# An output projection by one Strassen level, in two contraction phases, in a hybrid attention and pooling block

## The chip, the cores and the metric

The kernel runs on one core of one Trainium2 chip. The metric is the device time of one execution in microseconds; three runs of the kernel before gave 2625.17, 2625.77 and 2626.29, median 2625.77. A profiled execution of it, from which all rows below are taken, has a span of 2626.6 us.

## What is computed

One layer over 512 tokens of width 4096. A normalised input goes through one input projection; its columns feed a sparse attention (16 heads over a shared latent, the keys picked by an indexer) and a pooling mixer (4 groups). Each branch is multiplied by its own gate; the two are put side by side (4096 channels), go through the output projection, and the normalised result is added to the input:

```python
h = _rmsnorm(x, pre_norm[l])
z = jnp.einsum('bsd,de->bse', h, w_in[l])
q, c, qi, kix, wix, gate_a, pool_in, gate_b = _split_cols(z)
...
ya = _sparse_attention(q, c, qi, kix, wix, w_uk[l], w_uv[l], k_top).reshape(B, S, D_ATTN)
ya = ya * jax.nn.silu(gate_a)
yb = _multiscale_pool(pool_in, w_pool[l], pool_scale[l]) * jax.nn.silu(gate_b)
y = jnp.einsum('bse,ed->bsd', jnp.concatenate([ya, yb], axis=-1), w_out[l])
x = x + _rmsnorm(y, post_norm[l])
```

The output projection is the einsum with `w_out`: 512 x 4096 times 4096 x 4096.

## The kernel before

All large products are made in a split form. `split` (L57) writes a float32 tile as a high part (ACT cast) and a low part (DVE subtraction, source minus high part); `mm3` (L70) makes a product of two such pairs by three matmuls, high by high, high by low and low by high. `staged` (L61) loads a 128 x 512 tile of weights from HBM by the SP queue and splits it, four buffers deep.

Stages in order: a first projection of the latent and the indexer keys, while the normalised input `xh`, `xl` (32 row tiles of 512 tokens) is written to SBUF and kept; then groups of 128 output channels (`group`, L235), each 8 steps `q` of one staged tile and 12 matmuls of 512 moving columns. Between the steps the helper `bg` emits pieces of other work (indexer, top k, attention, mixer). Each finished 128-channel tile goes by `put` (L334) to `cat` in HBM; the last one stays in SBUF. The very last group is the gate of the pooling mixer, group 3, part 3, with 12 matmuls of the mixer's own map (`ymix`) among its 96.

The output projection stands in the last pool scope (L481 on). `reload` brings the 32 tiles of `cat` back and splits them into `ch`, `cl`, which take the SBUF places of `xh`, `xl`. `chunk(db, blocks)` handles 512 output columns: for each of 32 row tiles `e` it stages `wout[db, e]` and makes three matmuls for each block of 128 tokens. The tokens are the stationary side (128 columns), the weights the moving side (512 columns). The first five chunks do all four token blocks, the others two and two, so that blocks 0 and 1 can be normalised and stored (`finish`) while blocks 2 and 3 are still multiplied. At the end of a chunk ACT squares the result with a running sum (L506, `junk`), DVE multiplies it by the post norm (L509, `yg`). `fetch` loads x, `finish` computes the root of the mean and does the last multiply-add (L530) and the store (L531).

A scheduler in the tile framework sets the order of the instructions on each engine from the program, so the order of the code is not the order on an engine; each engine then runs its own list in order, waiting at semaphores. Weight loads of TensorE (rows PEld) stand beside the matmuls (rows PE).

Of the kernel before, what the change touches and what calls it, by code (L numbers as in the profile page):

```python
# [43 lines left out]
def block_kernel(ctx: ExitStack, tc: tile.TileContext, xT, x, gk, wc, wkw, wf, wuk, wuv, kvn,  # L44
# [44 lines left out]
    cat = dr.tile([NK, P, S], F32, name="cat")  # L89

# [144 lines left out]
    def group(gi, evac, per=1, t0=0):  # L235
# [98 lines left out]
    def put(e, src, scl, sg):  # L334
        V.scalar_tensor_tensor(sg, src, scl, sg, op0=ALU.mult, op1=ALU.mult)
        if e == NK - 1:
            split(sg, *[t[:, 1] for t in cat_tile(NK // 2 - 1)])
# [4 lines left out]

    def cat_tile(i):
        if i not in ct:
            ct[i] = (big.tile([P, 2, S], F32R, tag=f"h{i}", name=f"ch{i}"),
                     big.tile([P, 2, S], F32R, tag=f"l{i}", name=f"cl{i}"))
        return ct[i]

    def pool_group(pl, g):
# [36 lines left out]
        for d in range(4):  # L386
# [8 lines left out]
            group(G_GB + 4 * g + d, evac, 2 if d == 0 else 1)  # L395
# [84 lines left out]

    with tc.tile_pool(name="op", bufs=2, reuse_waits="tile") as opl:  # L481
        def reload(i):
            for j in range(2):
                if 2 * i + j < NK - 1:
                    raw = st.tile([P, S], F32, tag="raw", name="cat_raw")
                    nc.sync.dma_start(raw, cat[2 * i + j])
                    split(raw, *[t[:, j] for t in cat_tile(i)])

        yss = [opl.tile([P, 8], F32, name=f"yss{b}", bufs=1) for b in range(NB)]
        yg = {}  # L490

        def chunk(db, blocks, every=1):
            pg = opl.tile([P, 512], F32, name="pg", bufs=1)
            nc.sync.dma_start(pg, gpost[:, ts(db, 512)].to_broadcast([P, 512]))
            yp = [bank("acc" if i == 3 else "w") for i in range(len(blocks))]
            for e in range(NK):
                if db == 0 and e % 2 == 0 and e // 2 + 2 < NK // 2:
                    reload(e // 2 + 2)
                wo = staged(wout[db, e])
                for i, b in enumerate(blocks):  # L500
                    mm3(yp[i], tuple(t[:, e % 2, ts(b, P)] for t in ct[e // 2]), wo, e == 0, e == NK - 1)
                if e % every == 0:
                    bg.step()
            for i, b in enumerate(blocks):
                junk = opl.tile([P, 512], mybir.dt.bfloat16, name="junk", bufs=1)
                A.activation(junk, yp[i], AF.Square, accum_out=yss[b][:, db:db + 1])  # L506
                tag, n = ("yb", 2 * NFULL) if b >= 2 and db < NFULL else ("ya", 16)
                yg[b, db] = opl.tile([P, 512], F32, tag=tag, name="yg", bufs=n)
                V.tensor_mul(yg[b, db], yp[i], pg)  # L509

        xs = {}
# [108 lines left out]
```

## Time and profile before

| | before |
|---|---|
| median of 3 runs | 2625.77 us |
| span of the profiled execution | 2626.6 us |
| PE busy | 2587.6 us (99%), 11768 matmuls |
| PEld busy | 2147.4 us (82%) |
| DVE busy | 1176.9 us (45%) |
| ACT busy | 863.8 us (33%) |
| output projection, first to last matmul | 1902.45 to 2609.93 us |
| HBM traffic | 293.53 MB read, 16.52 MB written |

The page gives busy time by engine, the chain of work that ended last, and groups of instructions by line. A matmul's end is modelled and matmuls overlap, so their pace is read from the distance of their starts and not from their length. A wait matters where TensorE stands behind it; idle time of DVE or ACT by itself costs nothing.

### The profile page before, as it was taken

To read this page: it belongs to the slowest core of one execution; us is meant where nothing else is said; L and a number is where in the kernel's file an instruction comes from. 1 tells how busy PE (TensorE), PEld (TensorE's weight loads), DVE (VectorE), ACT (ScalarE), POOL (GpSimd) and SP (SyncE) were. 2 spreads that over 40 slices of the span, in tenths; PEclk is the share of its full clock that TensorE was granted. 3 is DMA by queue.
4 is the path that set the end of the run, shared out by engine and by line. 5 is a ranking of instruction groups with operands and counts; after the bars stand their busy time and mean duration, and the time that the engine had idled before them with its cause. 6 is when DMAs were issued, how large, how long until landed. Compare 5 with 4: busy or idle time off the path is not lost.

```text
span 2626.6 us, 31765 instructions
## 1 busy us (share of the span) xinstructions
PE 2587.6 (99%) x11768; PEld 2147.4 (82%) x11768; DVE 1176.9 (45%) x2086; ACT 863.8 (33%) x1542; POOL 46.7 (2%) x36
## 2 busy tenths in 40 slices
PE   7999999999999999999999999999999999999997
PEld 5799888888888888888888888888888888888875
DVE  9465783344344444444344334344452222235655
ACT  5344322233333333333332222222342222235443
POOL 5100000000000000000000000000000000000000
PEclk9999999999999999999999999999999999999998
DMA  6334333333333333333333333333473333346786
GB/s 202 99 100 109 96 100 107 103 92 90 98 94 92 89 97 92 92 93 92 94 93 97 106 106 96 105 104 101 129 224 101 101 97 103 101 133 197 224 284 220
DMA packets 169068, 312.15 MB, mean 119 GB/s; under 512 B 19536, under 2 KB 19664, under 8 KB 168912
## 3 DMA queue, kind: packets, MB, share of 16 engines
q1 hardware_dynamic: 168912, 310.12, 40.5%
q8 instruction: 92, 1.51, 0.2%
q14 instruction: 64, 0.52, 0.1%
HBM read 293.53 MB, written 16.52 MB: 118 GB/s over the span
## 4 chain that ended last, share of the span: by engine, by line
PE 90%; DMA 2%; DVE 1%; ACT 0%; issue 0%; DVEq 0%; SPq 0%; ACTq 0%
PE ps_acc L72 21%; PE ps_acc L74 20%; PE ps_acc L73 20%; PE ps_w L73 9%; PE ps_w L74 9%; PE ps_w L72 9%; DMA raw<-in_wout 2%; PE ps_w L447 1%; PE ps_w L279 1%; DVE lo L59 0%; DVE xr L530 0%; DMA xr<-in_x 0%; ACT hi L58 0%; DMA out<-xr 0%; DVE yg L509 0%
## 5 line engine op out<-in xcount | busy, mean ns | idle before, releaser
L59 DVE TENSOR_TENSOR lo<-raw,hi 128x512 fp32r<-128x512 f32 x1008 | 698.7, 695 | 1216.7 <-ACT hi L58 1143.2
L58 ACT CAST hi<-raw 128x512 fp32r<-128x512 f32 x1008 | 626.2, 622 | 1548.4 <-PE ps_acc L73 929.1
L72 PE MATMUL ps_acc<-xh,hi 128*128 128x512 f32 (+1 forms) x2304 | 893.0, 388 | 0.0
L74 PE MATMUL ps_acc<-xh,lo 128*128 128x512 f32 (+1 forms) x2304 | 883.9, 384 | 0.0
L73 PE MATMUL ps_acc<-xl,hi 128*128 128x512 f32 (+1 forms) x2304 | 883.7, 384 | 0.0
L72 PEld LDWEIGHTS ps_acc<-xh,hi 128*128 128x128 f32 x2304 | 432.7, 188 | 81.5 <-issue 2.2
L74 PEld LDWEIGHTS ps_acc<-xh,lo 128*128 128x128 f32 x2304 | 432.4, 188 | 81.4 <-issue 0.2
L73 PEld LDWEIGHTS ps_acc<-xl,hi 128*128 128x128 f32 x2304 | 433.0, 188 | 76.3
L73 PE MATMUL ps_w<-lo,ch 128*128 128x512 f32 x864 | 338.3, 392 | 3.3 <-DVE lo L59 3.2
L72 PE MATMUL ps_w<-hi,ch 128*128 128x512 f32 x864 | 337.2, 390 | 1.8 <-ACT hi L58 1.8
L74 PE MATMUL ps_w<-hi,cl 128*128 128x512 f32 x864 | 336.9, 390 | 0.0
L73 PEld LDWEIGHTS ps_w<-lo,ch 128*128 128x128 f32 x864 | 162.6, 188 | 41.8 <-DVE lo L59 8.3
L72 PEld LDWEIGHTS ps_w<-hi,ch 128*128 128x128 f32 x864 | 162.5, 188 | 36.7 <-ACT hi L58 2.7
L74 PEld LDWEIGHTS ps_w<-hi,cl 128*128 128x128 f32 x864 | 162.6, 188 | 33.4
L73 PE MATMUL ps_w<-lo,xh 128*128 128x512 f32 x128 | 52.9, 414 | 9.6 <-DVE lo L59 9.6
L72 PE MATMUL ps_acc<-hi,ch 128*128 128x512 f32 x160 | 62.2, 389 | 0.0
L73 PE MATMUL ps_acc<-lo,ch 128*128 128x512 f32 x160 | 62.2, 389 | 0.0
L74 PE MATMUL ps_acc<-hi,cl 128*128 128x512 f32 x160 | 62.2, 389 | 0.0
L72 PE MATMUL ps_w<-hi,xh 128*128 128x512 f32 x128 | 52.5, 410 | 7.1 <-ACT xh L58 6.4
L426 ACT ACTIVATE prob<-prob,nm 128x128 f32<-128x128 f32 (+1 forms) x64 | 36.1, 564 | 63.3 <-DVE nm L423 63.3
L74 PE MATMUL ps_w<-hi,xl 128*128 128x512 f32 x128 | 52.2, 408 | 0.0
L155 POOL TENSOR_TENSOR sumsq<-sumsq,sq 128x512 f32<-128x512 f32 x31 | 45.9, 1481 | 34.0 <-ACT sq L151 32.8
(180 smaller groups left out, 1601.3 us busy)
## 6 DMA issues: line engine op xcount, KB each, us to landing
raw<-in_wf SPq DMA_DIRECT2D x576, 256.0 KB, 2.6
raw<-in_wout SPq DMA_DIRECT2D x352, 256.0 KB, 2.9
raw<-in_wc SPq DMA_DIRECT2D x32, 256.0 KB, 2.7
xr<-in_x SPq DMA_DIRECT2D x32, 256.0 KB, 4.7
out<-xr SPq DMA_DIRECT2D x32, 256.0 KB, 2.3
cat_raw<-cat SPq DMA_DIRECT2D x31, 256.0 KB, 2.9
xt<-in_xT SPq DMA_DIRECT2D x15, 512.0 KB, 3.6
raw<-in_wpool SPq DMA_DIRECT2D x16, 256.0 KB, 2.6
```

Of the source, the lines that this page charges most:

```text
L58: A.copy(hi, src)
L59: V.tensor_sub(lo, src, hi.bitcast(F32))
L72: nc.tensor.matmul(dst, lh, rh, start=start, stop=False)
L73: nc.tensor.matmul(dst, lh, rl, start=False, stop=False)
L74: nc.tensor.matmul(dst, ll, rh, start=False, stop=stop)
L155: nc.gpsimd.tensor_add(sumsq, sumsq, sq)
L279: nc.tensor.matmul(dp[j][:, :n], lhs[j][x0], rhs[j][x1], start=i == 0, stop=i == 2)
L426: A.activation(pb, pb, AF.Exp, scale=-1.0, bias=nm, accum_out=sm)
L447: nc.tensor.transpose(tp[:, ts(b - s, P)], prob[:, OFF[b] + P * s:OFF[b] + P * s + P], ident)
```

## The change

The output projection is replaced. Tokens (512 = 2 x 256), contraction rows (pairs of 128-row tiles) and columns (512 = 2 x 256) are each cut in halves, and the 2 x 2 by 2 x 2 block product is made by 7 products of sums of blocks (one Strassen level, Winograd's form) in place of 8. The 16 pairs of row tiles are taken in two phases of 9 and 7 pairs (`KP`): phase 0 pairs tiles 0 to 8 with 9 to 17, phase 1 pairs 18 to 24 with 25 to 31. A phase goes over all 8 blocks of 512 columns.

- `operands(p, i)` loads two tiles of `cat`, makes four sums on DVE (256 columns each) and splits all seven operands into one tile `ops`, which lies where part of the normalised input was. For phase 0, `operands` 0 to 7 are emitted among the steps of the last group (`after`), the ninth behind it; for phase 1 in the last block of phase 0.
- `weights(p, db, i)` loads a 128 x 1024 tile of the four quadrants of `w_out`, makes four sums on DVE (512, 256 and 256 columns) and splits seven operands (512 and 1280 columns), two buffers deep, two steps ahead.
- A step is 7 products x 2 halves of 128 tokens x 3 matmuls of 256 moving columns into 7 PSUM banks. After the last step of a block ACT copies the banks to `pt`, and `collect` adds them up on DVE, spread over the next steps by `bg`. In phase 0 POOL stores the block to `part` in HBM; in phase 1 POOL adds the stored block back by two accumulating transfers (256 KB, then 768 KB), then ACT squares eight pieces (L564) and DVE scales.
- x is loaded in tiles of 128 x 2048 at the end of phase 1; the root and the last multiply-add stand behind the last `collect`, for all tokens; stores are 1 MB each.
- `put` writes every tile to `cat`; the input is kept in tiles of seven slots (`x_slot`) instead of pairs. The pool `st` is closed before the projection. On the host `wout` and `x` are laid out by quadrants.

```diff
-            h2 = big.tile([P, 2, S], F32R, tag=f"h{k2}", name=f"xh{k2}")
-            l2 = big.tile([P, 2, S], F32R, tag=f"l{k2}", name=f"xl{k2}")
...
-                split(gx, h2[:, j], l2[:, j])
-                xh.append(h2[:, j])
-                xl.append(l2[:, j])
+                xh.append(x_slot(2 * k))
+                xl.append(x_slot(2 * k + 1))
+                split(gx, xh[k], xl[k])
...
             if q == 7:
                 evac(z)
+            if after:
+                after(q)
             bg.step(per)
...
+    def operands(p, i, pool, tag=None, bufs=1):
+        e = 2 * (KP[0] * p) + i
+        w = pool.tile([P, 8, H], F32, tag=tag, name="cw", bufs=bufs)
+        q, s = w[:, 0:4], w[:, 4:8]
+        for j in range(2):
+            nc.sync.dma_start(q[:, 2 * j:2 * j + 2], cat[e + KP[p] * j].rearrange("p (a t) -> p a t", a=2))
+        V.tensor_add(s[:, 0], q[:, 1], q[:, 3])
+        V.tensor_sub(s[:, 2], q[:, 0], q[:, 1])
+        V.tensor_sub(s[:, 1], s[:, 0], q[:, 0])
+        V.tensor_sub(s[:, 3], q[:, 2], s[:, 1])
+        o = big.tile([P, 2, NSLOT // 2, H], F32R, tag=f"k{i}", name=f"ops{i}")
+        split(w[:, 0:3:2], o[:, 0, 0:2], o[:, 1, 0:2])
+        split(w[:, 3:8], o[:, 0, 2:7], o[:, 1, 2:7])
+        cat_ops[p, i] = o
...
+        def weights(p, db, i):
+            w = opl.tile([P, 8, H], F32, name="wr")
+            nc.sync.dma_start(w[:, 0:4], wout[KP[0] * p + i, db].rearrange("p (a c) -> p a c", a=4))
+            V.tensor_sub(w[:, 4:6], w[:, 1:3], w[:, 0:2])
+            V.tensor_sub(w[:, 6], w[:, 2], w[:, 4])
+            V.tensor_sub(w[:, 7], w[:, 3], w[:, 6])
+            hi = opl.tile([P, 7, H], F32R, name="wh")
+            lo = opl.tile([P, 7, H], F32R, name="wl")
+            split(w[:, 0:3:2], hi[:, 0:2], lo[:, 0:2])
+            split(w[:, 3:8], hi[:, 2:7], lo[:, 2:7])
+            return hi, lo
...
+            V.tensor_add(c0, pt[:, 0:1], pt[:, 1:2])
+            V.tensor_add(pt[:, 2], pt[:, 2], pt[:, 0])
+            yield
+            V.tensor_add(c[:, 0:2], pt[:, 3:5], pt[:, 2:3].to_broadcast([P, 2, 512]))
+            yield
+            V.tensor_add(c[:, 2], c[:, 0], pt[:, 4])
+            V.tensor_add(c[:, 0:2], c[:, 0:2], pt[:, 5:7])
+            yield
+            if p == 0:
+                nc.gpsimd.dma_start(part[db], t)
+                return
+            nc.gpsimd.dma_start(c0, part[db, :, 0:1], accum_op=ALU.add)
+            nc.gpsimd.dma_start(c, part[db, :, 1:4], accum_op=ALU.add)
...
+                A.activation(junk, slot[:, ts(i % 2, H)], AF.Square, accum_out=yss[:, i, db:db + 1])
...
+        order = [(p, db, i) for p in range(2) for db in range(NG) for i in range(KP[p])]
+        operands(0, 8, opl, "yo", 3)
+        staged_w = {n: weights(*order[n]) for n in range(2)}
+        for n, (p, db, i) in enumerate(order):
...
+            for (a, w), z in zip(PRODUCTS, banks):
+                for h in range(2):
+                    zz, ab = z[:, ts(h, H)], (o[:, 0, a, ts(h, P)], o[:, 1, a, ts(h, P)])
+                    nc.tensor.matmul(zz, ab[0], wh[:, w], start=i == 0 and h == 0, stop=False)
+                    nc.tensor.matmul(zz, ab[0], wl[:, w], start=False, stop=False)
+                    nc.tensor.matmul(zz, ab[1], wh[:, w], start=False, stop=i == KP[p] - 1 and h == 1)
+            if i == KP[p] - 1:
+                pt = opl.tile([P, 7, 512], F32, name="pt", bufs=1)
+                for j, z in enumerate(banks):
+                    A.copy(pt[:, j], z)
+                bg.add(collect(p, db, pt))
+            if n + 2 < len(order):
+                staged_w[n + 2] = weights(*order[n + 2])
+            if p == 0 and db == NG - 1 and i < KP[1]:
+                operands(1, i, opl, "yo", 3)
+            bg.step()
```

The list of PE is the same in both programs up to the first matmul of the projection. Three places on the engines that feed it follow; `raw`, `hi`, `lo` are a staged weight tile and its parts, `wr`, `wh`, `wl` the same of the changed kernel (one number per step), `cw` and `ops` the sources and parts of the operands.

DVE where the last group ends (`gate_z` is its result), before:

```order
L59 TENSOR_TENSOR cl3_15256<-cat_raw_15253,ch3_15255 128x512
L59 TENSOR_TENSOR cl3_15256<-cat_raw_15259,ch3_15255 128x512
L59 TENSOR_TENSOR lo_15266<-raw_15263,hi_15265 128x512
L330 TENSOR_TENSOR gate_z_15163<-ps_acc_14999,R_72 128x512
L59 TENSOR_TENSOR lo_15284<-raw_15281,hi_15283 128x512
L59 TENSOR_TENSOR cl4_15302<-cat_raw_15299,ch4_15301 128x512
L332 SCALAR_TENSOR_TENSOR sg_15162<-sg_15162,gate_z_15163 128x512
L59 TENSOR_TENSOR cl4_15302<-cat_raw_15305,ch4_15301 128x512
L335 SCALAR_TENSOR_TENSOR sg_15162<-ps_w_14998,psc_75,sg_15162 128x512
```

The same engine behind the gate, now, down to the first low part of the first step's weights:

```order
L63 TENSOR_TENSOR ops7_15239<-cw_15232,ops7_15239 128x512
L63 TENSOR_TENSOR ops6_15202<-cw_15195,ops6_15202 128x1280
L363 TENSOR_TENSOR cw_15232<-cw_15232 128x256
L63 TENSOR_TENSOR ops7_15239<-cw_15232,ops7_15239 128x1280
L361 TENSOR_TENSOR cw_15251<-cw_15251 128x256
L360 TENSOR_TENSOR cw_15251<-cw_15251 128x256
L362 TENSOR_TENSOR cw_15251<-cw_15251 128x256
L63 TENSOR_TENSOR ops8_15258<-cw_15251,ops8_15258 128x512
L363 TENSOR_TENSOR cw_15251<-cw_15251 128x256
L511 TENSOR_TENSOR wr_15263<-wr_15263 128x512
L63 TENSOR_TENSOR wl_15269<-wr_15263,wh_15268 128x512
```

Before, weights of the projection were split ahead of the gate; now operands 6 to 8 stand between the gate and the first weights.

ACT in the projection before, over the end of a chunk:

```order
L58 CAST hi_16557<-raw_16555 128x512
L58 CAST hi_16575<-raw_16573 128x512
L506 ACTIVATE junk_16515,yss0_15177<-ps_w_15935 128x512
L506 ACTIVATE junk_16519,yss1_15178<-ps_w_15936 128x512
L506 ACTIVATE junk_16523,yss2_15179<-ps_w_15937 128x512
L506 ACTIVATE junk_16527,yss3_15180<-ps_acc_15938 128x512
L58 CAST hi_16593<-raw_16591 128x512
```

ACT now, in the last block of phase 0, with the operands of phase 1:

```order
L62 CAST wh_18961<-wr_18956 128x512
L62 CAST ops2_18974<-cw_18967 128x512
L62 CAST wh_19027<-wr_19022 128x512
L62 CAST wh_18961<-wr_18956 128x1280
L62 CAST ops3_19040<-cw_19033 128x512
L62 CAST ops2_18974<-cw_18967 128x1280
L62 CAST wh_19092<-wr_19087 128x512
L62 CAST wh_19027<-wr_19022 128x1280
```

The casts of the operands stand between those of the weights, and twice the small cast of a step stands ahead of the large cast of the step before it.

ACT now, behind the end of a block of phase 1 (`k9` and `y0` are the results that the accumulating transfers write):

```order
L62 CAST wh_20155<-wr_20150 128x512
L62 CAST wh_20155<-wr_20150 128x1280
L564 ACTIVATE junk_20497,yss_15250<-k9_20222 128x256
L564 ACTIVATE junk_20499,yss_15250<-k9_20222 128x256
L62 CAST wh_20216<-wr_20211 128x512
L62 CAST wh_20216<-wr_20211 128x1280
L62 CAST wh_20272<-wr_20267 128x512
L564 ACTIVATE junk_20501,yss_15250<-y0_19747 128x256
L62 CAST wh_20272<-wr_20267 128x1280
L564 ACTIVATE junk_20503,yss_15250<-y0_19747 128x256
```

The squares read what a transfer wrote, and casts of later weights stand behind them; before, they read PSUM.

## Rows read from the trace of the kernel before

**Rows 1.** Page: busy us, share and count by engine; the chain's shares.

```profile
PE 2587.6 (99%) x11768; PEld 2147.4 (82%) x11768; DVE 1176.9 (45%) x2086; ACT 863.8 (33%) x1542; POOL 46.7 (2%) x36
PE 90%; DMA 2%; DVE 1%; ACT 0%; issue 0%; DVEq 0%; SPq 0%; ACTq 0%
```

**Rows 2.** Stages: us, busy of PE, PEld, DVE, ACT, POOL; clock; DMA.

```profile
1902.45:2450.00 547.55, 547.55 (x2417) 453.41 (x2416) 200.97 (x295) 181.66 (x317) 0.00 (x0) 1.00 0.47 135
2450.00:2609.93 159.93, 154.85 (x658) 123.07 (x656) 88.34 (x143) 71.63 (x123) 0.00 (x0) 0.99 0.78 246
2609.93:2626.60 16.67, 0.00 (x1) 0.00 (x0) 13.41 (x32) 1.14 (x5) 0.00 (x0) 0.57 0.65 252
```

**Rows 3.** Timeline of PE in the projection (start, length, what), 45 intervals apart.

```profile
2189.64 0.39 PE L73 MATMUL ps_w<-lo,ch 128*128 128x512 f32 x1
...
2199.84 0.39 PE L73 MATMUL ps_w<-lo,ch 128*128 128x512 f32 x1
```

**Rows 4.** Timeline of PE, then of PEld, in the attention.

```profile
516.65 0.28 PE L72 MATMUL ps_w<-kh,qh 128*128 128x256 f32 x1
516.77 0.28 PE L73 MATMUL ps_w<-kl,qh 128*128 128x256 f32 x1
516.89 0.28 PE L74 MATMUL ps_w<-kh,ql 128*128 128x256 f32 x1
517.01 0.40 PE L72 MATMUL ps_acc<-xh,hi 128*128 128x512 f32 x1
517.24 0.40 PE L73 MATMUL ps_acc<-xl,hi 128*128 128x512 f32 x1
...
516.77 0.19 PEld L74 LDWEIGHTS ps_w<-kh,ql 128*128 128x128 f32 x1
516.89 0.19 PEld L72 LDWEIGHTS ps_acc<-xh,hi 128*128 128x128 f32 x1
```

**Rows 5.** DVE groups by form: busy us, mean ns | idle before.

```profile
L59 DVE TENSOR_TENSOR lo<-raw,hi 128x512 fp32r<-128x512 f32 x1008 | 698.7, 695 | 1216.7 <-ACT hi L58 1143.2 <-PE ps_w L447 34.6 <-PE ps_w L73 33.5
L530 DVE SCALAR_TENSOR_TENSOR xr<-yg,ry,xr 128x512 f32<-128x512 f32 x32 | 22.7, 746 | 8.2 <-DMA xr<-in_x 8.2
L229 DVE TENSOR_TENSOR kd<-kt,ib 128x256 f32<-128x256 f32 x2 | 0.8, 424 | 0.1
```

**Rows 6.** Timeline of DVE: two instructions that do not depend on each other.

```profile
1853.45 0.69 DVE L330 TENSOR_TENSOR gate_z<-ps_acc,R 128x512 f32<-128x512 f32 x1 [1.60 <-PE ps_acc L74]
1854.06 0.68 DVE L59 TENSOR_TENSOR lo<-raw,hi 128x512 fp32r<-128x512 f32 x1
```

**Rows 7.** ACT groups by form.

```profile
L58 ACT CAST hi<-raw 128x512 fp32r<-128x512 f32 x1008 | 626.2, 622 | 1548.4 <-PE ps_acc L73 929.1 <-PE ps_acc L74 278.3 <-issue 89.0
L506 ACT ACTIVATION_READ_ACCUMULATOR junk<-ps_w 128x1 f32 x27 | 5.2, 194 | 0.0
L58 ACT CAST kwh<-kwr 128x640 fp32r<-128x640 f32 x4 | 2.9, 722 | 0.0
```

**Rows 8.** DMA issues (KB each, us to landing); landing times of `xr`.

```profile
raw<-in_wout SPq DMA_DIRECT2D x352, 256.0 KB, 2.9
xt<-in_xT SPq DMA_DIRECT2D x15, 512.0 KB, 3.6
...
DMA to landing us min/median/max: 2.0/4.2/6.9
```

**Rows 9.** Timeline of PE at a wait, and the stage behind it.

```profile
2573.52 0.50 PE L72 MATMUL ps_w<-hi,ch 128*128 128x512 f32 x1 [1.64 <-ACT hi L58]
...
2574.60:2577.40 2.80, 2.80 (x8) 2.22 (x7) 1.59 (x3) 1.80 (x3) 0.00 (x0) 0.52 0.82 244
```

**Rows 10.** Timeline of the tail.

```profile
2610.75 0.69 DVE L509 TENSOR_TENSOR yg<-ps_w,pg 128x512 f32<-128x512 f32 x1
...
2612.74 0.75 DVE L530 SCALAR_TENSOR_TENSOR xr<-yg,ry,xr 128x512 f32<-128x512 f32 x1
...
2613.52 10.34 SPq L531 DMA_DIRECT2D out<-xr  x16
```

More of the change, by code (lines that the diff above doesn't have):

```diff
@@ L89, in block_kernel, with x_slot @@
     cat = dr.tile([NK, P, S], F32, name="cat")
+    part = dr.tile([NG, P, 4, 512], F32, name="part")
+    slots = {}
+    def x_slot(i):
+        t, j = divmod(i, NSLOT // 2)
+        if t not in slots:
+            n = min(NSLOT // 2, 2 * NK - i)
+            slots[t] = big.tile([P, n, S], F32R, tag=f"k{t}", name=f"xk{t}")
+        return slots[t][:, j]
     xh, xl = [], []
@@ L233, in block_kernel, with group @@
         split(tp, *kT)
-    def group(gi, evac, per=1, t0=0):
+    def group(gi, evac, per=1, t0=0, after=None):
         z = bank("acc")
@@ L394, in evac @@
                 put(16 + 4 * g + d, yp, psc[:, 4 * g + d:4 * g + d + 1], sg)
-            group(G_GB + 4 * g + d, evac, 2 if d == 0 else 1)
+            last = g == 3 and d == 3
+            group(G_GB + 4 * g + d, evac, 2 if d == 0 else 1,
+                  after=(lambda q: operands(0, q, pl, "cw", 2)) if last else None)
     V.tensor_scalar(psc, psc, 0.5, None, op0=ALU.mult)
@@ L479, in block_kernel @@
     inner.close()
+    st_stack.close()
     with tc.tile_pool(name="op", bufs=2, reuse_waits="tile") as opl:
[L482 to L509, printed above, removed]
@@ L551, in block_kernel @@
[L551 to L557 removed]
+        PRODUCTS = ((0, 0), (1, 2), (4, 5), (5, 4), (3, 3), (2, 6), (6, 1))
+        def weights(p, db, i):
[9 more added lines that the diff above has]
+            return hi, lo
@@ new lines, in block_kernel @@
+        xs = []
+        for db in range(NG):
+            pool, tag, n = (big, f"k{db + 1}", 1) if db < 6 else (opl, "wr", 2)
+            xs.append(pool.tile([P, 4, 512], F32, tag=tag, name=f"xr{db}", bufs=n))
+            nc.sync.dma_start(xs[db], x[db])
+        bg.drain()
+        ry = opl.tile([P, 2, 2], F32, name="ry", bufs=1)
+        ms = opl.tile([P, 2, 2], F32, name="yms", bufs=1)
+        ysum = opl.tile([P, 8], F32, name="ysum", bufs=1)
+        V.tensor_reduce(ysum, yss, axis=AX.X, op=ALU.add)
@@ new lines, in block_kernel @@
+        tot = ysum.rearrange("p (a b) -> p a b", a=2)
+        V.tensor_add(ms, tot[:, 0].rearrange("p (a b) -> p a b", a=2), tot[:, 1].rearrange("p (a b) -> p a b", a=2))
+        V.tensor_scalar(ms, ms, 1.0 / D, EPS, op0=ALU.mult, op1=ALU.add)
+        rsqrt(opl, ms, ry, "yms_t")
+        for db in range(NG):
+            c0, c = ys[db]
+            t = xs[db]
+            for b in range(2):
+                r = [ry[:, h, b:b + 1] for h in range(2)]
+                s = ts(b, H)
+                V.scalar_tensor_tensor(t[:, 0, s], c0[:, 0, s], r[0], t[:, 0, s], op0=ALU.mult, op1=ALU.add)
+                V.scalar_tensor_tensor(t[:, 2, s], c[:, 1, s], r[0], t[:, 2, s], op0=ALU.mult, op1=ALU.add)
+                V.scalar_tensor_tensor(t[:, 1:4:2, s], c[:, 0:3:2, s], r[1], t[:, 1:4:2, s], op0=ALU.mult, op1=ALU.add)
+            nc.sync.dma_start(out[db], t)
@@ L578, in tiles, with quads @@
         return m.reshape(NK // n, n, P, -1).transpose(0, 2, 1, 3).reshape(NK // n, P, -1)
+    def quads(m):
+        out = []
+        for p in range(2):
+            t = m[2 * KP[0] * P * p:][:2 * KP[p] * P].reshape(2, KP[p], P, NG, 2, H)
+            t = np.stack([t[0, ..., 0, :], t[0, ..., 1, :], t[1, ..., 1, :], t[1, ..., 0, :]], axis=3)
+            out.append(t.transpose(0, 2, 1, 3, 4).reshape(KP[p], NG, P, 4 * H))
+        return np.concatenate(out)
     x0 = np.asarray(x)[0]
```

111 lines of the change are left out of this document (54 added, 57 removed).

## The prediction

> **What bounds the kernel now.** I read the busy shares and the chain that ended last, then the stages, then single matmuls, then the engines that feed them. PE is busy 99% of the span and 90% of the chain is matmuls [rows 1]: only TensorE time, or a wait put in front of TensorE, moves the end. By stages [rows 2]: the output projection runs from 1902.45 to 2609.93, 707.5 us. Up to 2450 PE is never idle while DVE is busy 201 of 547.6 us and ACT 182; behind that PE loses some microseconds; behind the last matmul lies a tail of 16.7 us. A matmul of 512 columns starts every 0.2267 us (45 intervals between the two rows, 10.20 us) [rows 3], so 3072 of them are 696.3 us and waits cost 11.2. The profiled span is 2626.6 us, the median of the runs 2625.77: I sum against the span and take off 0.8.
>
> **1. The matmuls.** Each of 128 steps (8 column blocks, 16 pairs of row tiles) has 7 products x 2 halves x 3 = 42 matmuls of 256 columns: 5376 for 3072, with an eighth fewer columns and 75% more weight loads. The attention stage shows this shape: from 516.65 to 517.24 lie three of 256 columns and one of 512, so 0.59 - 0.227 = 0.363, or 0.121 each, and the starts stand 0.12 apart [rows 4]. I take 0.120: 645.1 us, 5.04 us a step. The ends are 0.1133, half of a 512 (609 us), and 0.121 (650). Fed without a wait, the stage is **62.4 us shorter**.
>
> The Trainium skill (TensorE: Matmul & The Clock Gate, Back-to-back issue gap) gives 262 cycles at 2.4 GHz for 256 columns, 0.109 us; by it the sum would be 587 us, 58 less. The 0.12 of [rows 4] decides against it.
>
> **2. The feeding.** `weights` gives DVE subtractions of 512, 256 and 256 columns and low parts of 512 and 1280. By 0.695 for 512 and 0.424 for 256 [rows 5], 1.06 per 1000 columns more, 1280 is 1.51 and 1024 is 1.24: 3.75 us a step. Independent DVE instructions start 0.61 apart though each lasts 0.69 [rows 6], 0.08 less each: 3.35. ACT casts 512 and 1280: by 0.622 for 512 and 0.722 for 640 [rows 7], 1.22 for 1280: 1.84. Both lie under PE's 5.04. The buffers are two deep, so the casts for step n+2 begin when step n ends: 0.62 + 1.22 + 1.51 = 3.4 us, against the 5.04 + 0.72 until the second product of n+2 needs the large part. The cover is 2.4 us a step. `collect` adds 0.70 + 0.70 + 1.24 + 0.70 + 1.24 = 4.6 (4.2 overlapped) once in a block and uses it up over two steps. I charge 0.25 for each of 8 blocks of the first phase: **+2** (ends 0 and 8).
>
> **3. The seam with the last group.** Nine operand tiles are built by DVE: four of 256, then 512 and 1280, 3.9 us or 3.4 overlapped, 30 in all, while the group has 108 matmuls of 512, 24.5 us, and they may only overwrite inputs that PE has finished with. In the listed order the group's own low parts come in time (operands 0 to 3 stand between them, and the last `lo` of the group is done 18.2 us after its first matmul). Operands 4 to 8 (17 us), three instructions of the gate (2) and about 1.7 us of waits for ACT's casts and the reloads (2.9 us each, [rows 8]) come before `wl` of the first step: 18.2 + 17 + 2 + 1.7 = 39, while PE is through at 24.5. PE then has 29 matmuls until the large low parts at 44.6; 55 of the first 84 remain, so it is done at 51.2 instead of 34.6: 16.6 us. Where PE idled 1.64 us before, the granted clock fell to 0.52, the 1.2 GHz level, in the 2.8 us behind [rows 9]: 2.8 at half pace loses 1.4, more after a long idle. **+19** (ends 12 and 25). Before, nothing is lost here.
>
> **4. The second phase's operands.** In the last block of phase one DVE has 3.35 + 3.4 = 6.75 us a step for seven steps against 5.04: 12 us, less the cover of 2.4. ACT's order also holds two inversions, as the one shown above: the small cast of a step, which waits until PE has freed its buffer two steps back, stands before the large cast of the step ahead of it, so PE waits 0.62 + 1.22 + 1.51 - 0.84 = 2.5 at each. Walked row by row the seven steps lose 0.8, 3.3, 2.5, 2.5, 2.5 and 1.5, less 0.7 and less 0.1 a step for the longer step: 12, and 2 for the clock: **+14** (ends 6 and 20).
>
> **5. The accumulating transfers.** In phase two POOL adds the stored 256 and 768 KB to the block. Nothing in the trace is issued by POOL or accumulates. A plain 256 KB takes 2.9 us, 512 KB 3.6, and under load up to 6.9 [rows 8]: 768 KB is 4.3 at the least; if the old values are read too it moves as 1.5 MB, 2.9 + 5 x 0.7 = 6.4; at the worst some 10. ACT is in order: the third square waits for it, and the large cast of the next weights stands behind that square, then DVE's low part, then PE. L550 ends 12.2 us behind the start of a block's last step; the square must start by 21.0 - 1.51 - 1.22 - 0.5 = 17.8. So 5.5 us are hidden. With 6.4 PE waits 0.9, and 0.5 once more behind the other five squares (each 0.42 for 256 columns, by the slope of the casts, and 0.19 for reading the sum, less overlap, [rows 7]): 1.4 in seven blocks: **+10** (ends 0 and 38).
>
> The Trainium skill (DMA: Bandwidth & Descriptors, Anatomy of one DMA) fits 2.0 us plus bytes over 436 GB/s to a transfer on this path: 3.8 us for 768 KB, by which this term were nothing. No row here shows the path.
>
> **6. The last block** loads eight 1 MB tiles of x beside the last weights. Before, PE lost nearly all of its 11.2 us in the stretch in which x came in, behind 2450 [rows 2], where a transfer of the x tiles took up to 6.9 us to land [rows 8]. **+3** (ends 0 and 8).
>
> **7. The tail.** From the last matmul on: copy and last adds 2.3 us, accumulation under load 8.5, six squares 2.9, scaling 1.2, root 1.5 (1.3 before, from 2611.44 to 2612.74, [rows 10]): 16.4. Then 8 tiles, each of two instructions of 512 columns (0.75, [rows 5]) and four of 256 (0.27 less), 2.9 overlapped: 23.4, with 8.4 MB to write. The last 16 tiles of before, 4.2 MB, took from 2613.5 to 2626.6, 320 GB/s [rows 10]; so the writes need 26.2 from the first on (19.8) and end at 46, with the close 47. Before it is 16.7 [rows 2]. **+30** (ends 22 and 38).
>
> **Sum:** -62.4 + 2 + 19 + 14 + 10 + 3 + 30 = +15.6: 2642.2 in the profile, 2641 as a median.
>
> **Rivals.** (a) *The accumulation is slow.* At 10 us each of seven blocks loses (10 - 5.5) + 0.4 = 4.9, 34 for 10, and the tail 3 more: 2668. For it: ACT's order, and no row at all for this kind of transfer. Against it: 256 KB land in 2.9. Chance 0.17.
> (b) *The covers hold.* Terms 2, 5 and 6 are nothing and term 4 is 7: 2641 - 2 - 10 - 3 - 7 = 2619, at the border of 0.2% (5.3 us, about what a measurement of this kernel tells from no change). For it: DVE was 37% busy, and the sums lie under 5.04. Chance 0.21.
> (c) *Faster: a 256-column matmul runs at half the price of a 512,* 0.1133, wherever weights follow each other in one stream. The first interval in [rows 4] allows it, the 512 behind the triple, 0.23, and the 0.363 in all speak against it. 5376 x 0.0067 = 36 less: 2605. It decides from a pace of 0.117, where 15.6 us are won back. Chance 0.10. The skill's 262 cycles, above, is this rival's rule.
> (d) *Weight loads bound.* PEld is busy 82% [rows 1] with 0.19 us for a load. If loads could not overlap, 5376 x 0.188 = 1011 us: +366, 3007. But the two loads in [rows 4] start 0.12 us apart, as the matmuls do. Chance 0.02. The Trainium skill (Perfetto Trace Analysis, Identifying the Most-Contended Engine) wants TensorE's headroom judged by this busy share; by it the change has none, and the row differs.
>
> **How the numbers follow.** The forecast, 2631 to 2656, has 0.50; (a) 0.17, (b) 0.21, (c) 0.10, (d) 0.02. Slower by over 0.2%: 0.47 of the forecast, (a) and (d): 0.66. Within: 0.03 of it and 0.13 of (b): 0.16. Faster: 0.08 of (b) and (c): 0.18. The range leaves out most of (c), the upper part of (a), and (d): 2612 to 2672.
>
> **What would show it.** In the new profile: 256-column matmuls 0.120 apart where PE is not idle (term 1; 0.113 is rival c, 0.188 is d). PE idle some 15 us behind the last `ps_acc<-xh` group, ended by DVE `wl`, with DVE busy throughout (3). PE idle 2 to 3 us in each of about five steps in the middle of the projection (4). ACT `junk` waiting for a transfer of POOL, and PE behind it, once per block in the second half (5): none is rival b, 4 us or more is a. About 47 us between the last matmul and the end, half of them with `out` transfers (7). The forecast is wrong if the pace is below 0.117, if DVE starts the operands earlier than its order lets me think, or if the squares wait much longer than 1 us.

## The result: 0.8% slower, and the profile after

The changed kernel takes 2646.4 us (median of 4 runs, 2644.1 to 2649.1) against 2626.0 of the kernel before on the same chip: 1.0078 times, 95% interval 1.0064 to 1.0092. The forecast was 2641, in a range of 2612 to 2672. The profiled execution has a span of 2642.3 us (the sum had 2642.2) and is the fastest of the four runs; the median lies 2.3 above it. In the runs of both kernels that have both numbers, the device time lies 1.8 to 1.9 us above the span. The profiled execution of before, with its span of 2626.6, was therefore one of some 2628.4 us (an estimate), 2.4 above its median. The account below, span against span, therefore finds 15.7 us; the medians are 20.4 apart.

First the busy line of the page, to be held against [rows 1]:

```profile
PE 2541.7 (96%) x14072; PEld 2220.2 (84%) x14072; DVE 1478.7 (56%) x2506; ACT 953.4 (36%) x1619; POOL 65.3 (2%) x60
```

PE does 46 us less work and yet the kernel is longer: its share fell from 99 to 96%. Where it stands still is seen by stages (columns as in [rows 2]). The first line is the time between the last matmul of the last group and the first of the projection, the fourth most of the last block of phase 0 (2237.6 to 2291.4) and of the first step of phase 1, the fifth the rest of phase 1, the last the tail:

```profile
1900.33:1913.20 12.87, 0.16 (x1) 0.00 (x0) 11.24 (x20) 5.62 (x7) 0.00 (x0) 0.60 0.72 239
1913.20:1920.00 6.80, 5.18 (x21) 4.59 (x22) 6.75 (x12) 4.19 (x4) 0.00 (x0) 0.50 0.02 6
1920.00:2240.00 320.00, 319.49 (x2647) 319.08 (x2647) 249.23 (x349) 138.32 (x176) 3.42 (x6) 0.99 0.37 127
2240.00:2295.00 55.00, 49.06 (x379) 46.03 (x377) 54.77 (x90) 30.50 (x39) 0.53 (x1) 1.00 0.46 157
2295.00:2595.59 300.59, 284.48 (x2333) 280.99 (x2333) 239.33 (x336) 155.21 (x276) 13.50 (x16) 1.00 0.51 151
2595.59:2642.30 46.71, 0.15 (x2) 0.00 (x0) 29.78 (x62) 6.21 (x20) 0.86 (x1) 0.54 0.66 241
```

The pace of the matmuls is read as in [rows 3], from two starts 84 intervals apart (timeline of PE):

```profile
2099.73 0.28 PE L588 MATMUL ps_w<-wh,ops 128*128 128x256 f32 x1
...
2109.81 0.28 PE L588 MATMUL ps_w<-wh,ops 128*128 128x256 f32 x1
```

That is 0.1200 us each, and 5261 of the 5375 intervals of the stage are 0.12. Since the pace is so even, every step of 42 matmuls has a fixed price of 5.04 us, and what a step takes beyond it is its loss. All losses below are worked out in this way, from the starts; they hold the idle time and what the matmuls behind it lose. The seam is the place where the last group ends and the projection begins. The account of the span against the 2626.6 us of before:

| term | forecast | measured |
|---|---|---|
| 1. 5376 matmuls at 0.120 in place of a stage of 707.5 | -62.4 | -62.4 |
| 2. sums of the blocks of phase 0 | +2 | +0.4 |
| 3. seam: 12.9 standing, 6.5 in the first five steps | +19 | +19.4 |
| 4. operands of phase 1: 8.5 in the last block of phase 0, 2.2 in the step behind | +14 | +10.7 |
| 5. accumulating transfers, seven blocks | +10 | +19.7 |
| 6. x loads in the last block | +3 | 0 |
| 7. tail, 46.7 in place of 16.7 | +30 | +30.0 |
| the last group ended earlier, at 1900.3 in place of 1902.5 | 0 | -2.1 |
| sum | +15.6 | +15.7 |

The terms agree far less well than their sum: 10 us too little in one place, and 8 too much in three, besides an early end of the group that cannot be put down to the change (the same stretch ended between 1900.6 and 1902.7 in the kernels below).

**The seam**, timelines of SP, ACT, PE and DVE:

```profile
1905.14 0.32 SPq L350 DMA_DIRECT2D cat<-sg  x1
1905.51 0.93 SPq L359 DMA_DIRECT2D cw<-cat  x2
1906.48 0.91 SPq L510 DMA_DIRECT2D wr<-in_wout  x2
...
1912.53 0.62 ACT L62 CAST wh<-wr 128x512 fp32r<-128x512 f32 x1 [1.80 <-DMA wr<-in_wout]
...
1913.20 0.58 PE L588 MATMUL ps_w<-wh,ops 128*128 128x256 f32 x1 [12.71 <-ACT wh L62]
1913.25 0.42 DVE L363 TENSOR_TENSOR cw<-cw 128x256 f32<-128x256 f32 x1
1913.59 0.69 DVE L511 TENSOR_TENSOR wr<-wr 128x512 f32<-128x512 f32 x1
1914.19 0.68 DVE L63 TENSOR_TENSOR wl<-wr,wh 128x512 fp32r<-128x512 f32 x1
...
1914.93 0.58 PE L589 MATMUL ps_w<-wl,ops 128*128 128x256 f32 x1 [0.93 <-DVE wl L63]
```

PE's first wait is ended by the cast of the first weights, and that by the load of the weights, which SP issued only at 1906.5: it stands behind the store of the last tile of `cat`, which waits for the gate. But only two matmuls run then; the third needs the first low part and waits for DVE. DVE comes to the weights from the last operand set without standing still, so it did not wait for the load: its list alone puts the end of the first low part at 1914.9. The load, there by 1912.5, is a second path, about a microsecond shorter. Behind the wait the granted clock is 0.50, the 1.2 GHz level, and matmuls start 0.213 apart in place of 0.120, some 30 of them.

**A block of phase 1** (the fifth; step 3's wait), timelines of DVE, POOL, ACT and PE in order of time:

```profile
2449.94 1.22 DVE L550 TENSOR_TENSOR y<-y,pt 128x1024 f32<-128x1024 f32 x1
...
2451.45 0.86 POOL L556 DMA_DIRECT2D y<-part  x1 [6.23 <-DVE y L550]
...
2458.32 0.42 ACT L564 ACTIVATE junk<-y 128x256 bf16<-128x256 f32 x1 [3.07 <-DMA y<-part]
2458.64 0.19 ACT L564 ACTIVATION_READ_ACCUMULATOR junk<-y 128x1 f32 x1
2458.73 1.25 ACT L62 CAST wh<-wr 128x1280 fp32r<-128x1280 f32 x1
...
2460.01 1.49 DVE L63 TENSOR_TENSOR wl<-wr,wh 128x1280 fp32r<-128x1280 f32 x1 [3.89 <-ACT wh L62]
...
2461.55 0.39 PE L589 MATMUL ps_w<-wl,ops 128*128 128x256 f32 x1 [1.09 <-DVE wl L63]
```

The square waits 3 us for the transfer, the cast behind it is ready and waits too, then DVE, then PE. One step later the same happens once more, since the other squares and DVE's scales have pushed back the next weights (ACT itself now stands 1.5 us for DVE's subtraction, which comes behind the scale):

```profile
2462.96 1.22 DVE L569 TENSOR_TENSOR y<-y,gp 128x1024 f32<-128x1024 f32 x1
2464.09 0.42 DVE L513 TENSOR_TENSOR wr<-wr 128x256 f32<-128x256 f32 x1
...
2464.54 1.26 ACT L62 CAST wh<-wr 128x1280 fp32r<-128x1280 f32 x1 [1.48 <-DVE wr L513]
```

How long the large transfer takes is the last line of the view of line 556 (issue to landing; the longest is that of the last block, which has the x loads beside it); the 256 KB one of line 555 has a median of 4.5.

```profile
DMA to landing us min/median/max: 6.8/6.8/9.0
```

**The tail**: the last block's transfer, the squares, the first multiply-add, the eight stores.

```profile
2598.54 0.86 POOL L556 DMA_DIRECT2D y<-part  x1 [3.67 <-DVE y L550]
...
2607.60 0.42 ACT L564 ACTIVATE junk<-y 128x256 bf16<-128x256 f32 x1 [4.26 <-DMA y<-part]
...
2613.88 0.48 DVE L622 SCALAR_TENSOR_TENSOR xr<-y,ry,xr 128x256 f32<-128x256 f32 x1
...
2616.90 20.69 SPq L625 DMA_DIRECT2D out<-xr  x8
```

### The profile page after: what moved, and what is told of

Its sections match the earlier page's. It is cut to its first block, busy times and chain, and to the rows that moved or that the text cites. A ratio compares the mean times of both kernels' runs of the same rounds, so it can differ in the third digit from the quotient of the medians.

```text
span 2642.3 us, 35860 instructions
## 1 busy us (share of the span) xinstructions
PE 2541.7 (96%) x14072; PEld 2220.2 (84%) x14072; DVE 1478.7 (56%) x2506; ACT 953.4 (36%) x1619; POOL 65.3 (2%) x60
## 5 line engine op out<-in xcount | busy, mean ns | idle before, releaser
L63 DVE TENSOR_TENSOR lo<-raw,hi 128x512 fp32r<-128x512 f32 x656 | 456.4, 696 | 821.4 <-ACT hi L62 748.2
L76 PE MATMUL ps_acc<-xk,hi 128*128 128x512 f32 (+1 forms) x2304 | 893.0, 388 | 0.0
L78 PE MATMUL ps_acc<-xk,lo 128*128 128x512 f32 (+1 forms) x2304 | 883.9, 384 | 0.0
L77 PE MATMUL ps_acc<-xk,hi 128*128 128x512 f32 (+1 forms) x2304 | 883.8, 384 | 0.0
L76 PEld LDWEIGHTS ps_acc<-xk,hi 128*128 128x128 f32 x2304 | 432.7, 188 | 81.3 <-issue 2.2
L78 PEld LDWEIGHTS ps_acc<-xk,lo 128*128 128x128 f32 x2304 | 432.5, 188 | 81.5 <-issue 0.3
L77 PEld LDWEIGHTS ps_acc<-xk,hi 128*128 128x128 f32 x2304 | 433.0, 188 | 76.4
L589 PE MATMUL ps_w<-wl,ops 128*128 128x256 f32 x1536 | 436.8, 286 | 21.1 <-DVE wl L63 20.9
L588 PE MATMUL ps_w<-wh,ops 128*128 128x256 f32 x1536 | 430.4, 285 | 15.8 <-ACT wh L62 15.7
L590 PE MATMUL ps_w<-wh,ops 128*128 128x256 f32 x1536 | 433.7, 284 | 0.0
L63 DVE TENSOR_TENSOR wl<-wr,wh 128x512 fp32r<-128x512 f32 (+1 forms) x256 | 276.9, 1087 | 89.3 <-ACT wh L62 88.6
L589 PEld LDWEIGHTS ps_w<-wl,ops 128*128 128x128 f32 x1536 | 295.5, 192 | 26.9 <-DVE wl L63 26.7
L588 PEld LDWEIGHTS ps_w<-wh,ops 128*128 128x128 f32 x1536 | 292.9, 193 | 17.9 <-ACT wh L62 17.5
L590 PEld LDWEIGHTS ps_w<-wh,ops 128*128 128x128 f32 x1536 | 295.7, 192 | 0.0
```

What stands on the lines that cost most here:

```text
L63: V.tensor_sub(lo, src, hi.bitcast(F32))
L76: nc.tensor.matmul(dst, lh, rh, start=start, stop=False)
L77: nc.tensor.matmul(dst, lh, rl, start=False, stop=False)
L78: nc.tensor.matmul(dst, ll, rh, start=False, stop=stop)
L588: nc.tensor.matmul(zz, ab[0], wh[:, w], start=i == 0 and h == 0, stop=False)
L589: nc.tensor.matmul(zz, ab[0], wl[:, w], start=False, stop=False)
```

## The experiments

Each kernel is the changed one with one edit, unless it says otherwise. Times are medians, beside the 2646.4 us of the change.

### 1. The squares later

```diff
-            yield
-            yield
-            for i in range(8):
...
+            if p and db and i in (3, 4):
+                if i == 3:
+                    with tc.issue_after(cast[order[n + 1]][0]):
+                        squares(db - 1, range(4))
+                    with tc.issue_after(cast[order[n + 2]][0]):
+                        squares(db - 1, range(4, 8))
+                else:
+                    with tc.issue_after(cast[order[n + 1]][1]):
+                        scales(db - 1)
```

`cast` holds the large cast and the large low part of each step's weights; what stands under `issue_after` is queued behind that instruction on its engine, with no other wait.

> The squares and scales of a block of phase 1 are queued behind the casts and low parts of steps 2 and 3 of the next block, so that the accumulating transfer has landed before ACT comes to them; nothing else moves. After the change the seven blocks that follow lose 19.7 us of PE time, two waits of about 1.3 us in steps 3 and 4 of each. Theory A (ACT stands in order behind the 768 KB transfer, 6.8 us): the loss falls to 3 us or less, the time by 15 to 18, to about 2629. Theory B (DVE has too much to do when the sums and scales of a block fall due, or the transfers slow the weight loads): the work is the same, so at least 12 of the 19.7 us stay, and the time falls by less than 7.

Measured: 2630.8 us, 15.5 less, 1.0016 times the kernel before (1.0007 to 1.0025). Phase 1 loses 3.1 us in place of 19.7 (not counting the first step), and nothing at all from the fourth block on. Waits of PE from 2300 to 2592 (us, times, longest), first of the change, then of this kernel:

```profile
PE ps_w L589 <- DVE wl L63: 15.0, 15, 1.7
```

```profile
PE ps_w L593 <- DVE wl L63: 2.0, 3, 1.1
```

DVE does the same work and the transfers are the same; what stands behind what on ACT and DVE was changed (and the post norm's tile has a second buffer). So the order was the cause, and not DVE's load. The run moves the squares on ACT and the scales on DVE together and does not tell what each is worth.

### 2 and 3. The seam: DVE's operands, SP's queue

```diff
-                  after=(lambda q: operands(0, q, pl, "cw", 2)) if last else None)
+                  after=(lambda q: q < LASTOP and operands(0, q, pl, "cw", 2)) if last else None)
...
-        operands(0, 8, opl, "yo", 3)
         staged_w = {n: weights(*order[n]) for n in range(2)}
...
+            if n in (0, 2, 4):
+                operands(0, LASTOP + n // 2, opl, "yo", 3)
```

`LASTOP` is 6. The third kernel has this and one more line, where `q` is POOL for the last tile:

```diff
-        nc.sync.dma_start(cat[e], sg)
+        (q or nc.sync).dma_start(cat[e], sg)
```

> At the seam the operands 6, 7 and 8 are built behind the weights of the first steps (one set after steps 0, 2 and 4) and no longer ahead of them; the store of the last tile of cat stays ahead of the first weight load on SP. After the change PE stands 12.9 us and the seam costs 19.7 in all. Theory A, that of the prediction (DVE's operand work ahead of the first low part is what PE waits for): 10 us of DVE work go from there, so the seam costs about 9 to 10, and the time falls by 9 to 11. Theory B (SP: the first weight load is queued behind the store, which waits for the gate): the load is issued at about 1904.3 in place of 1906.5 and has less beside it, PE begins at about 1908.5, the seam costs 14 to 16, and the time falls by 4 to 6.

> As e2_seam_order, and besides the last store of cat is issued by POOL, so that on SP nothing stands between PE's last matmul of the group and the first weight load. Theory B (SP): the load is issued at about 1900.5 and lands near 1904, PE begins at about 1905, the seam costs 9 to 11 us, 4 to 5 less than in e2_seam_order. Theory A (DVE): the same time as e2_seam_order within 1.5 us.

Measured: 2643.8 and 2640.3 us. The seam costs 14.2 us without the operands ahead of the weights and 10.9 with the store on POOL as well (19.4 in the change), each in one profile; the medians fell by 2.6, which is no more than the spread of the runs, and by another 3.4. PE's first matmul and the first load, in the second kernel (with DVE's first instruction on the weights) and then in the third:

```profile
1906.75 0.86 SPq L511 DMA_DIRECT2D wr<-in_wout  x2
...
1910.70 0.69 DVE L512 TENSOR_TENSOR wr<-wr 128x512 f32<-128x512 f32 x1 [4.40 <-DMA wr<-in_wout]
...
1911.42 0.58 PE L588 MATMUL ps_w<-wh,ops 128*128 128x256 f32 x1 [9.01 <-ACT wh L63]
```

```profile
1899.11 3.05 SPq L512 DMA_DIRECT2D wr<-in_wout  x2
...
1904.61 0.45 PE L589 MATMUL ps_w<-wh,ops 128*128 128x256 f32 x1 [2.59 <-ACT wh L63]
1906.82 0.58 PE L590 MATMUL ps_w<-wl,ops 128*128 128x256 f32 x1 [1.54 <-DVE wl L64]
```

Both edits help, by 5.2 and 3.3 us of seam. With DVE's 10 us gone DVE itself stands 4.4 us for the load and PE 9; with the load early PE stands 2.6, and DVE's share shows as the wait behind it. DVE's work taken away alone brings half of the 9 to 11 us of theory A, because the path of the load, hidden behind DVE's in the change, comes out.

### 4. The operands' sums on POOL

```diff
-        V.tensor_add(s[:, 0], q[:, 1], q[:, 3])
+        E = nc.gpsimd if p else V
+        E.tensor_add(s[:, 0], q[:, 1], q[:, 3])
...
```

The three other sums go the same way.

> The four sums of each operand set of phase 1 (256 columns each) are made by POOL and no longer by DVE, which takes 1.36 us of 3.4 off DVE for each of the seven sets; the casts on ACT and their order stay. After the change the last block of phase 0 and the first step of phase 1 lose 10.7 us. Theory A (DVE's throughput: 6.75 us of work a step against 5.04 of PE): DVE has 5.4 a step, the loss falls to 2 to 4 us and the time by 6 to 9. Theory B, the prediction's second reason (inversions on ACT, small casts ahead of large ones): the loss stays at 8 or more. Theory C (POOL's adds, about 0.8 us each by the 1.49 us of its 512-column adds, make DVE slower beside them or come late): the loss grows.

Measured: 2659.4 us, 13 more. The last block of phase 0 loses 17.0 us in place of 8.5. POOL's adds of 256 columns, then DVE's instructions in the same microseconds:

```profile
2252.54 0.73 POOL L361 TENSOR_TENSOR cw<-cw 128x256 f32<-128x256 f32 x1
2253.35 1.96 POOL L363 TENSOR_TENSOR cw<-cw 128x256 f32<-128x256 f32 x1
2255.39 1.85 POOL L364 TENSOR_TENSOR cw<-cw 128x256 f32<-128x256 f32 x1
```

```profile
2254.64 2.02 DVE L63 TENSOR_TENSOR wl<-wr,wh 128x1280 fp32r<-128x1280 f32 x1
2256.58 1.21 DVE L512 TENSOR_TENSOR wr<-wr 128x512 f32<-128x512 f32 x1
```

An add takes 0.73 us while DVE waits, and 1.9 beside a busy DVE; DVE's low part takes 2.02 in place of 1.49, its subtraction of 512 columns 1.21 in place of 0.69. The Trainium skill (Advanced Engine Details and Errata, GPSIMD Details) says that POOL shares a read and a write interface with DVE, in conflict with DVE instructions of two SBUF inputs; all of these are such, and the trace agrees. So theory C, and the question between A and B stays for the next two. Not all of the 13 us is the price of the two engines side by side: the largest single loss, 7.1 us in the block's third step, follows POOL's first add of the stretch, which took 5.2 us while ACT stood at the cast behind it and DVE at ACT.

### 5. One operand set in every second step

```diff
-            if p == 0 and db == NG - 1 and i < KP[1]:
-                operands(1, i, opl, "yo", 3)
+            if n in SPREAD:
+                operands(1, SPREAD.index(n), opl, "yo", 3)
```

`SPREAD` is 63, 65 and so on to 75; the last block of phase 0 begins at step 63, phase 1 at 72.

> The seven operand sets of phase 1 are built one in every second step, from the first step of the last block of phase 0 to the fourth of phase 1, all on DVE as in the change. Theory A (DVE's throughput): over the last block DVE has 9 x 3.35 + 5 x 3.4 + 4.2 for the block's sums = 51.4 us against 45.4 of PE and a cover of 2.4, then 4 x 3.35 + 2 x 3.4 + 4.2 = 24.4 against 20.2: 3.6 + 4.2, so 6 to 8 us are lost where the change lost 10.7 (58.2 of work in nine steps against 45.4 and 2.4, 10.4), and the time falls by 3 to 5. Theory B (inversions on ACT): with a step between two sets ACT has time to come back, at most 2 us are lost, and the time falls by 8 or more.

Measured: 2646.9 us, no change. The last block of phase 0 and the first of phase 1 lose 5.7 us in place of 11.0, a little under the 6 to 8 of theory A; but the time, which both theories had falling, did not, for the three blocks behind lose 14.9 in place of 9.3 (10.0 to 12.0 in the profiles of experiments 2, 3, 6, 7 and 8, which leave these blocks as they are). In the first of them the squares stand ahead of the large casts of two steps, and ACT stands at them for the small transfer, which was issued no later than in the change:

```profile
2331.23 0.42 ACT L565 ACTIVATE junk<-y 128x256 bf16<-128x256 f32 x1 [3.52 <-DMA y<-part]
```

DVE is also late with this block's sums: its large transfer is issued 13.3 us into the next block, in place of 8.1. What one place gained was paid at the next, at the wait that experiment 1 takes away; experiments 1 and 9 bear that out.

### 6. No operands for phase 1

```diff
-                operands(1, i, opl, "yo", 3)
...
-            o = cat_ops[p, i]
+            o = cat_ops[0, i]
```

> Leaves out the operands of phase 1: its steps use those of phase 0, so the second half of the contraction is made with the wrong left factor; the matmuls, weights, sums, transfers and squares stay. In the change the last block of phase 0 loses 8.5 us and the first step of phase 1 another 2.2. Theory A (these seven sets put DVE at 58.2 us of work in nine steps of 45.4): both losses go, at most 0.5 us stay there, and the time falls by 9 to 11, to about 2636. Rival (what is lost there belongs to the turn of the phases itself, the block's sums and the store of the part): at least 4 of the 10.7 us stay. The later blocks keep their 2.5 us each by both.

The kernel leaves out the seven operand sets of phase 1 and multiplies those of phase 0 once more. Measured: 2637.1 us, 9.3 less. In the last block of phase 0 and the step behind not one interval is longer than 0.12. The stage, to be held against the fourth line of the change's table (DVE 54.77 of 55.00 there):

```profile
2240.00:2290.00 50.00, 50.00 (x419) 50.00 (x418) 40.65 (x57) 21.10 (x27) 0.53 (x1) 1.00 0.38 124
```

The whole of the 10.7 us belongs to the seven sets. That it is DVE's work and not the order on ACT, the run alone does not show, since the sets' casts went too; the busy row does: with the sets DVE has work in 54.8 of 55 us, ACT in 30.5, so DVE had no time in which to wait for a cast that came late.

### 7. The first weights early

Experiment 3's edits, and the first step's weights loaded and split ahead, with their high and low parts in 14 KB beside the last groups' pool:

```diff
+    w0p = w0_stack.enter_context(tc.tile_pool(name="w0p", bufs=1, side="right", reuse_waits="tile"))
...
-        staged_w = {n: weights(*order[n]) for n in range(2)}
+        staged_w = {0: first_w[0], 1: weights(*order[1])}
```

> As e3_seam_store, and besides the seven operands of the first step's weights are loaded and split long before, into 14 KB beside the pool of the last groups, so that PE goes from the last group into step 0 without a wait. Theory B (weights on their way, and the clock lost by standing still): only step 1's weights still come from behind the group, some 2 to 3 us late; the granted clock stays at the upper level; the seam costs 3 to 6 us in place of 19.4, the time falls by 13 to 16, to about 2632. Rival (DVE: operands 6 to 8 are still owed and must be made in steps 0 to 4): the seam still costs 9 or more, as in e3_seam_store (10.9).

Measured: 2637.2 us, 9.2 less. PE goes into the projection without a wait, and the clock stays:

```profile
1900.00:1920.00 20.00, 18.92 (x147) 17.90 (x145) 18.46 (x32) 9.76 (x13) 0.75 (x1) 1.00 0.61 204
```

The first block loses 2.9 us and the two behind it 3.3, in place of 19.4 and 0.4: 13.6 us less, as expected. The time fell by only 9. In this execution phase 1 lost 24.7 us to the transfers (19.7 in the change's profile, 21 to 23 in those of experiments 2, 3 and 6): what the transfers cost differs from profile to profile. Whether that is the execution or the kernel is not shown, with one profile of each.

### 8. The tail

```diff
+            if (p, db, i) == (1, NG - 1, 0):
+                c0, c = ys[db] = y_home(db)
+                nc.sync.dma_start(c0, part[db, :, 0:1])
+                nc.sync.dma_start(c, part[db, :, 1:4])
...
+                V.tensor_add(c[:, 0], c[:, 0], pt[:, 5])
+                V.tensor_add(c[:, 1], c[:, 1], pt[:, 6])
```

The last two lines are the only sums that need the last products.

> For the last block alone the stored part is loaded back by plain transfers during the block, into the place that its result takes, and DVE adds it, with all sums that do not need the last two products ahead of the last matmul: no accumulating transfer behind the last matmul. After the change the tail is 46.7 us, 18.3 of them before the first store's multiply-add, and 9 of these the transfer. Theory A (the tail is a chain of transfer, squares, root, then stores of 8.4 MB): the chain before the first multiply-add falls to 7 to 9 us, the tail to 36 to 38, the time by 9 to 11. Rival (the loads of x, which end late, or the stores bind): the tail stays above 43, since the end is set by other transfers; or the loads of the part hold up the weights on SP, and PE loses in the last block what the tail gains.

Measured: 2645.9 us. The tail falls to 38.5 us, 8.2 less, and the last block loses 6.8 in place of 2.5; more in the other places of this execution took the rest. In the last block the loads of the part run beside the accumulating transfer of the block before, which takes 10.1 us in place of 6.8, and ACT stands at its squares:

```profile
2578.70 0.42 ACT L582 ACTIVATE junk<-yo 128x256 bf16<-128x256 f32 x1 [6.45 <-DMA yo<-part]
```

### 9 and 10. All that helped, together

> All that helped together: late squares, the early first weights with the last store on POOL and late operands 6 to 8, operand sets of phase 1 spread, the last block's part loaded back ahead. By the terms as measured or expected: 2646.4 - 16 (late squares) - 14 (seam) - 3 (spread) - 10 (tail) = 2603, 0.9% under the kernel before. Rival (the waits are not separate: DVE has 3.35 us of work in each step of 5.04, and what is taken from one place comes back at the next): the sum falls short by more than a third, 2618 or more.

Measured: 2607.1 us (2606.1 to 2609.3), **0.9924 times the kernel before** (0.9912 to 0.9937), 39 less than the change. The projection and the tail:

```profile
1901.69:2567.90 666.21, 652.99 (x5377) 646.88 (x5375) 557.66 (x799) 334.14 (x502) 17.16 (x23) 1.00 0.47 146
2567.90:2606.13 38.23, 0.16 (x2) 0.00 (x0) 31.64 (x65) 5.41 (x16) 0.00 (x0) 0.53 0.69 282
```

The stage is 666.2 us in place of 707.5, with 21.1 of loss over its 645.1: 7.6 in the first three blocks, 11.3 from the last block of phase 0 to the fourth of phase 1, 2.2 in the last. The gains add up to 39 of the 43 expected. With the spread sets the stretch of 11.3 had lost 20.7 in experiment 5, 13.8 in experiment 1 and 20.3 in the change: spreading pays once the squares no longer wait, by 2.5 us between two profiles (13.8 and 11.3).

The tenth kernel sends the last block's loads by POOL's queue:

```diff
-                nc.sync.dma_start(c0, part[db, :, 0:1])
-                nc.sync.dma_start(c, part[db, :, 1:4])
+                nc.gpsimd.dma_start(c0, part[db, :, 0:1])
+                nc.gpsimd.dma_start(c, part[db, :, 1:4])
```

> As e8_all, but the part of the last block is loaded back by POOL's queue and not by SP's. In e8_all PE lost 2.2 us in the last block, in e7_tail 6.8. If the loads hold up the weights because they stand between them on SP, the last block loses 0 to 0.5 us here and the time falls by about 2, to 2605. If it is the 1 MB itself, moved beside the weights, the loss stays at 2 and the time does not move. It can also be worse: the accumulating transfer of the block before stands on POOL behind the loads, and its squares come later.

Measured: 2608.2 us, the same within the spread of the runs; the last block loses 2.5. SP's queue is not what holds it up there. The wait begins at the load of a step's weights, here in the ninth kernel:

```profile
2549.05 0.69 DVE L539 TENSOR_TENSOR wr<-wr 128x512 f32<-128x512 f32 x1 [4.98 <-DMA wr<-in_wout]
```

The x loads alone do not do it: in experiment 1 they are issued in the last block too, DVE stands 1.8 us for that load, and the block loses nothing. What comes on top here is the part's 1 MB (and one load of the post norm); whether the part alone would do was not tried.

## Why the prediction was right, and where it was not

**Direction and size** came from the right account: a stage 62 us shorter, against a seam, a change of phases, a transfer and a longer tail. The range held and the distance to the forecast is 5 us: 2.3 because the median lies above the profiled execution, and 2.6 because a device time lies 1.8 above its span where the prediction took off 0.8. Those 0.8 are no property of the program: the profiled execution of before lay some 2.4 above its median, and the prediction set its span beside the median of other runs. That the sum of the terms met the new span within 0.1 us is luck twice over: four terms and the end of the group were off and cancel, and one profiled execution lies below the median of its kernel, the other above. Median against median the change cost 20.4 us; the 4.7 us beyond the account lie in executions that left no profile, and their place is not known.

**Term 1** held to the digit: 0.120, read from a triple in the attention [rows 4]. Rival (c) asked for 0.1133 and (d) for 0.188; neither is seen. PEld is busy in 319.1 of the 320 us of the third stretch, since each load takes 0.19 us and one starts every 0.12, and PE keeps its pace; so the busy share of the loads was no bound here.

**Term 2** was a charge for a cover that held: one wait of 0.4 us in all of phase 0 up to its last block.

**Term 3** has the right size, and its walk along DVE's list came out: it put the first low part some 14.5 us behind the end of the group and the large one 20.1, and in the profile they ended 14.5 and 20.0 behind it. What it left out is the second path, right behind DVE's. PE's first wait ended with the load of `wr`, 6 us after its issue (3.4 us at its quickest), behind the store on SP's queue, and not with `wl`, as the prediction's sign had it. In the change this cost nothing more, but it halves what a cure of DVE brings: experiment 2 took the operands away and left 14.2 us, experiment 3 took the store away too and left 10.9. That the clock falls behind such a wait [rows 9] was right.

**Term 4** took 12 us from a walk with two inversions on ACT, and 2 for the clock. The clock stayed at 1.00, and experiment 6 and the busy table give DVE's work as the cause; the two inversions, at which DVE would have had to wait for ACT, do not show (DVE stood still for ACT once in that block, for 0.2 us). The plain sum gives the size, if the sums of the block before are put in, which the prediction left out: 9 x 3.35 + 7 x 3.4 + 4.2 = 58.2 us of DVE work in nine steps of 45.4, less the cover of 2.4, is 10.4.

**Term 5** was the mis-sized one: 1.4 us a block forecast, 2.5 and more measured. The transfer was nearly right (6.4 forecast, 6.8 measured), and so was the first wait: 0.9 forecast, 1.1 of idle in the rows above. What failed is the second wait, put at 0.5: the six squares, and the scales that stand on DVE ahead of the next subtraction of weights, make it nearly as long as the first. Experiment 1 shows that the order on the two engines is to blame. Rival (a), 10 us for the transfer, came true only beside other large transfers (9.0 in the last block, 10.1 in experiment 8).

**Term 6** was nothing: the last block lost 2.5, as most of those before it, and 0 in experiment 1.

**Term 7** has the right size, but the path that gave it did not set the end. The first multiply-add came after 18.3 us (16.4 forecast). From there the prediction let the writing of 8.4 MB end last. In the profile DVE sets the pace, with 1.45 us of work for each half of a tile: the eight stores are issued 2.9 us apart, each lands 3.8 to 3.9 us after its issue, and the last is issued at 2637.3. All stores landed in the same time, so none was held up by the one before, and that the tail still came to 46.7 us is luck.

## What to carry over

A wait does not cost what it lasts but what stands behind it on its engine: put an instruction that waits for a transfer behind the work that the next stage needs, and most of the wait is gone, as the 15.5 us of experiment 1 show. When a change moves PE work to DVE, add up DVE's work over each stretch with all of its parts, and look at every queue at a seam (SP's too), since a second path can stand close behind that of the busiest engine. Terms that come out right in sum can be wrong one by one, and only the account by places shows what to mend: here it led from 0.8% slower to 0.8% faster.

## What the runs showed of the hardware

- A matmul of 256 columns with a weight load of its own starts 0.1200 us behind the one before at the upper clock level, and 0.213 at the lower. The ratio is 1.78 and not 2: at a column a cycle 256 columns take 0.2133 us at 1.2 GHz and 0.1067 at 2.4, so that 0.013 us come on top at the upper level alone. The 512 columns of [rows 3] show the same 0.013 (0.2267 against 0.2133).
- An accumulating transfer from HBM into SBUF takes 4.5 us for 256 KB and 6.8 for 768 KB, and up to 10.1 beside other large transfers; plain loads of 512 KB in the same kernel take 3.6.
- POOL and DVE slow each other when both add tiles in SBUF: 0.73 to 1.96 us for an add of 256 columns on POOL, 0.69 to 1.21 for 512 on DVE. POOL's very first add after a long pause took 5.2 us; why was not tried.
